# A hybrid decoder layer: the S5 setup's steps ordered behind the projection's own work on VectorE and SyncE

## The chip, the cores and the metric

The kernel runs on one core of a Trainium2 chip. The metric is the device time of one execution in microseconds (us); the number that counts is the median over runs. The core has a matrix engine (TensorE, PE in the profile, with PEld for its weight loads), three engines for elementwise work (VectorE = DVE, ScalarE = ACT, GpSimd = POOL) and SyncE (SP), which here only issues DMA transfers. Each engine runs its instructions strictly in the order of its own queue; what an instruction needs from another engine it waits for with a semaphore, and everything behind it on its queue waits too.

## The reference, cut to what matters

The layer normalises `x` (2048 tokens of 1024), projects it with one wide weight, and feeds three branches whose results are gated, projected, merged and added to `x`:

```
h = rms_norm(x, norm_w);  proj = h @ w_in
(u_a, z_a, q, k, v, z_b, xbc, dt, z_c, gate_logits) = split(proj)
y_a = s5_mixer(u_a, ...) * silu(z_a)              # diagonal complex state space model
y_b = attention_mixer(q, k, v, ...) * silu(z_b)   # 3 groups of dilated window attention
y_c = ssd_mixer(xbc, dt, z_c, ...)                # Mamba-2
merged = sum_i sigmoid(gates_i) * (y_i @ proj_i)
out = x + merged @ w_out
```

The S5 branch needs tables that depend on the parameters alone, not on `x`. The step that prepares them starts as

```
step = exp(log_step);  mag = exp(a_re * step);  ang = a_im * step
lam_re, lam_im = mag * cos(ang), mag * sin(ang)
bb = f(lam, a) * b         # (32 groups, 64 states, 16 channels), complex
```

and goes on to powers of `lam`, products with `b` and `c`, and their layout in DRAM.

## The kernel before

The projection is the first stage. `main_qkv` (L421 to L443) goes through ten weight groups of 256 columns, in the order q0, k0, v0, q1, k1, v1, q2, k2, v2, z. For each it loads 1 MB of weights (`wr`, one buffer; L370), casts it to a high part on ScalarE (`wh`, L385) and forms the low part on VectorE (`wl`, L386), in four pieces each (`wh_q_0` to `wh_q_3`). Then come four units; a unit is 48 matmuls of 128x256 (L398 to L400: high by high, low by high, high by low), three for each of 8 slices of the contraction and two token tiles, so that the pieces 0 to 3 of `wh` and `wl` are wanted one after the other. A unit's result goes from PSUM (three buffers) to SBUF by a ScalarE copy; q and k are then normalised by `head_norm` (L445 to L455: copy and square on ScalarE, sum on VectorE, two power operations on GpSimd, a multiplication on VectorE, L454), v is only copied, z gets a SiLU. A store on SyncE's queue (L442) ends the unit, and its instruction is kept in `self.anchor`. The units are numbered from 1: q0 has 1 to 4, k0 5 to 8, v0 9 to 12, q1 13 to 16, k1 17 to 20, v1 21 to 24, q2 25 to 28, k2 29 to 32, v2 33 to 36, z 37 to 40.

Beside the units other work is generated in steps. `run` takes jobs as (generator, steps, first unit, last unit) and advances each after every unit by the share that is due. In the first forty units two jobs run: `s5_setup` and `a0_early`, which normalises the second half of the tokens (`x` loads L280, `xj`, `xs`, `x`, L289 to L295, `xe`).

`s5_setup` (L1063 to L1235) loads the S5 parameters (`s5ld`, `s5prm`, `s5b`, L1075 to L1087), transposes two of them on TensorE (`s5pt`, L1079), computes exponentials, sine and cosine on 128x32 tiles, powers (`s5pw`, `s5wr`, `s5w`, L1102 to L1148), the `bb` products (`s5bb`, L1158 to L1160), loads and scales `c` (`s5c`, L1166 to L1169), transposes it on TensorE (`s5ct`, L1173) and copies it out (`s5d`, L1175), and builds two levels of phases (`s5ph`, L1182 to L1221). `put` (L1083) writes the tables to `tab_d` in DRAM: 2048 rows of 32 floats, thus 128 bytes a row and 256 KB a put, nine puts in all. The generator has fifteen points at which it yields. Its memory (a pool named `jp0`) is given back when unit 40 has been generated; attention's first loads (`qb`, `kb`, `vb`, L797) and the next step of S5, `s5_tables` (L1241 to L1306: `s5ks`, `s5x`, `s5k`, `s5o`, `s5w`, and the store `o_d<-s5o`, L1289), use the same memory, and so wait for the last put to have landed.

What is generated is not what runs. A list scheduler orders each engine's queue from a model of the time line, and may take an instruction of a step earlier than the units around it wherever its data and memory allow. `issue_after(ins)` limits that: all instructions made under it stand behind `ins` if they are on the same engine as `ins`. It orders a queue and adds no semaphore.

Of the kernel before, what the change touches and what calls it, by code (L numbers as in the profile page):

```python
# [21 lines left out]
P = 128  # L22
# [127 lines left out]
class Hybrid:  # L150
# [294 lines left out]
    def head_norm(self, nm, ps, e):  # L445
        nc = self.nc
        sq = self.ev(f"sq_{nm}")
        ss = self.gp.tile([P, 2, 8], F32, name=f"ss_{nm}", tag="hss", bufs=3)
        nc.scalar.copy(e, ps)
        e8 = e.rearrange("p a (h d) -> p (a h) d", d=64)  # L450
        nc.scalar.activation(sq.rearrange("p (h d) -> p h d", d=64), e8, AF.Square)
        nc.vector.reduce_sum(ss[:, 0, :], sq.rearrange("p (h d) -> p h d", d=64), axis=AX.X)
        self.rsqrt(ss[:, 1, :], ss[:, 0, :], 8, 1.0 / 64, EPS)
        nc.vector.tensor_mul(e8, e8,  # L454
                             ss[:, 1, :].unsqueeze(2).to_broadcast([P, 8, 64]))  # L455

    def silu2(self, nm, z, out, zin=None):

# [1083 lines left out]
    def main(self):  # L1542

        first = []
        for half, order in enumerate(((self.main_qkv, self.main_dtz, self.main_xbc, self.main_uz, self.main_gates),
                                      (self.main_uz, self.main_qkv, self.main_dtz, self.main_xbc, self.main_gates_plain))):
            for f in order:
                first.append((f, half))
        def early(gen, n):
            for _ in range(n):  # L1550
                yield next(gen)

        def chain(*gens):
            for g in gens:
                yield from g

        def steps(jobs):
            done = [0] * len(jobs)
            alive = [True] * len(jobs)

            def advance(u):
                for i, (g, n, a, b) in enumerate(jobs):
                    want = n * (u - a + 1) / (b - a) if u >= a else 0
                    while alive[i] and (done[i] < want or u >= b):
                        try:
                            next(g)
                            done[i] += 1
                        except StopIteration:
                            alive[i] = False
            return advance  # L1570

        def open_pool(name):
            st = ExitStack()
            return st, st.enter_context(self.tc.tile_pool(name=name, bufs=1, side="right"))

        def run(jobs, until):

            nonlocal u
            adv = steps(jobs)
            while u < until:  # L1580
                if next(units, 0) is None:
                    u += 1
                    adv(u)
                else:
                    break
            adv(10 ** 6)

        def all_units():
            for k, (f, half) in enumerate(first):
                if k == 0:  # L1590
                    self.a0()
                    self.consts()
                elif k == 5:
                    self.a0_late(3)
                yield from f(half)

        u, units = 0, all_units()
        st, self.jp = open_pool("jp0")
        ssd0, early0 = self.ssd(0), self.a0_early()
        run([(self.s5_setup(), 18, 2, 38), (early(early0, 6), 6, 20, 40)], 40)  # L1600
        st.close()
        tb, self.tp = open_pool("tp")
        st, self.jp = open_pool("jp1")
        tabs = self.s5_tables()
        run([(chain(self.attention(0, 0), self.attention(1, 0)), 40, 41, 79), (early(tabs, 54), 54, 41, 80),
             (self.ssd_dt(0, self.jp), 3, 73, 79), (early0, 3, 40, 52)], 80)
        st.close()
        sums = self.sums(0)
        run([(tabs, 10, 80, 86), (early(sums, 4), 4, 81, 85)], 85)
        run([(tabs, 10, 80, 86), (sums, 5, 85, 88)], 88)  # L1610
        tb.close()
        st, self.sp = open_pool("sp0")
        run([(ssd0, 65, 89, 135)], 136)
        st.close()
        st, self.jp = open_pool("jp2")
        run([(self.s5(), 42, 153, 180)], 180)
        st.close()
        st, self.jp = open_pool("jp2g")
        run([(self.s5_glu(), 25, 181, 196), (self.ssd_dt(1, self.jp), 2, 196, 198)], S5END)
        st.close()  # L1620
        self.jp = self.left_pool("jp3")
        st, self.op = open_pool("op")
        ssd, merge = self.ssd(1), self.merge()
        att = chain(self.attention(0, 1), self.attention(1, 1), self.attention(2, 1))
        run([(early(att, 46), 46, S5END + 2, 236), (self.out_weights(), 20, S5END + 3, 234)], 236)
        st.close()
        self.late = [None, None]
        self.late[0], self.sp = open_pool("sp1")
        run([(att, 26, 236, ATTEND), (early(ssd, 11), 11, 237, ATTEND)], ATTEND)
        self.close_left()  # L1630
        self.late[1], self.mp = open_pool("mp")
        run([(early(merge, 4), 4, ATTEND, 272), (early(ssd, 6), 6, ATTEND, 272)], 10 ** 6)
        self.close_left()
        self.rest = [merge, ssd]
# [51 lines left out]
```

## Time and profile before

| what | value |
|---|---|
| median of 3 runs (lowest, highest) | 2504.53 us (2504.11, 2505.44) |
| the profiled execution's own time | 2510.43 us |
| its span, first to last instruction | 2508.4 us |
| TensorE busy | 2426.4 us, 97% |
| weight loads / VectorE / ScalarE / GpSimd busy | 85% / 57% / 33% / 29% |
| mean granted TensorE clock | 0.988 |
| chain that ended last | PE 68%, DMA 12%, DVE 10%, POOL 3%, SP's queue 3%, ACT 2% |

The profiled execution took 2.0 us more than its span and 5.9 us more than the median. TensorE is busy nearly throughout, so a change in a stage can be seen in two places only: in TensorE's idle time (the view of waits, with what ended each wait) and in the granted clock (the view of windows, where 1.00 is 2.4 GHz and 0.50 is 1.2 GHz). A row of a timeline gives the start, the busy time, the engine and line, and in square brackets the idle time before it with what ended that.

### The profile page before, as it was taken

The numbers are of one execution on the slowest core, as the hardware profiler recorded it, in microseconds if no ns is written. First come the engines' busy times: TensorE is split into PE (matmuls) and PEld (weight loads), VectorE is DVE, ScalarE is ACT, GpSimd is POOL, SyncE is SP. The second block draws the span as 40 slices with busy tenths as digits, with TensorE's granted clock in tenths as the row PEclk, the third lists the DMA queues.
The fourth block names the chain that finished last, engine by engine and source line by source line (L and its number), as shares of the span: only waits on it lengthen the run. The fifth ranks groups of instructions, "written<-read, shape, count | busy, mean of one in ns | idle before, by whom it ended". The sixth has DMA issues, their size and how long they took to land.

```text
span 2508.4 us, 40680 instructions
## 1 busy us (share of the span) xinstructions
PE 2426.4 (97%) x15072; PEld 2126.8 (85%) x15072; DVE 1436.5 (57%) x3104; ACT 836.6 (33%) x1780; POOL 722.8 (29%) x785
## 2 busy tenths in 40 slices
PE   8989999999999999999999999999999799999999
PEld 8989998788788888988999978878888578898888
DVE  6953467876767672577664566632334886552321
ACT  4223334543444343222243355542332312120100
POOL 2242233543344540245331000010110465422120
PEclk9999999999999999999999999999999899999999
DMA  7764543454544456466544567783343689898886
GB/s 165 111 166 139 163 124 128 139 168 131 155 140 123 125 170 195 113 183 169 156 154 140 166 204 211 239 269 106 114 130 108 209 281 314 292 304 292 297 285 221
DMA packets 449734, 457.65 MB, mean 182 GB/s; under 512 B 115585, under 2 KB 389505, under 8 KB 442369
## 3 DMA queue, kind: packets, MB, share of 16 engines
q1 hardware_dynamic: 449536, 455.06, 59.0%
q8 instruction: 119, 1.95, 0.3%
q14 instruction: 79, 0.64, 0.1%
HBM read 306.90 MB, written 148.06 MB: 181 GB/s over the span
## 4 chain that ended last, share of the span: by engine, by line
PE 68%; DMA 12%; DVE 10%; POOL 3%; SPq 3%; ACT 2%; issue 2%; ACTq 0%; DVEq 0%; POOLq 0%
PE fp L1500 3%; PE fp L1501 3%; PE fp L1502 3%; PE ps_g L410 3%; PE ps_g L409 3%; PE ps_g L411 3%; PE ao L874 2%; PE ps_uz L409 2%; PE ps_uz L411 2%; PE ps_uz L410 2%; PE op L1531 2%; PE op L1532 2%; PE op L1533 2%; PE psx_g L722 2%; PE psx_g L720 2%
## 5 line engine op out<-in xcount | busy, mean ns | idle before, releaser
L1013 POOL TENSOR_TENSOR sr<-tle,ahl 128x384 fp32r<-128x384 f32 x128 | 126.6, 1008 | 483.9 <-PE sd L1018 400.4
L1501 PE MATMUL fp<-fy_lo,fp 128*128 128x512 f32 x384 | 154.4, 402 | 6.5 <-DVE fy_lo L1473 6.5
L1500 PE MATMUL fp<-fy_hi,fp 128*128 128x512 f32 x384 | 156.7, 409 | 0.0
L409 PE MATMUL ps_g<-hT_hi,wh_g 128*128 128x512 f32 x384 | 155.4, 405 | 0.0
L410 PE MATMUL ps_g<-hT_lo,wh_g 128*128 128x512 f32 x384 | 154.3, 402 | 0.0
L411 PE MATMUL ps_g<-hT_hi,wl_g 128*128 128x512 f32 x384 | 154.1, 401 | 0.0
L1502 PE MATMUL fp<-fy_hi,fp 128*128 128x512 f32 x384 | 153.7, 400 | 0.0
L1531 PE MATMUL op<-fo,fm_hi 128*128 128x256 f32 x512 | 146.1, 286 | 4.7 <-DMA fo<-wo_d 4.7
L1505 POOL TENSOR_TENSOR fm<-fm,fg 128x512 f32<-128x512 f32 x64 | 86.7, 1355 | 218.1 <-DVE fg L1503 153.4
L1532 PE MATMUL op<-fo,fm_hi 128*128 128x256 f32 x512 | 144.8, 283 | 0.0
L1533 PE MATMUL op<-fo,fm_lo 128*128 128x256 f32 x512 | 144.5, 283 | 0.1
L409 PE MATMUL ps_xbc<-hT_hi,wh_xbc 128*128 128x512 f32 x320 | 130.0, 406 | 0.0
L411 PE MATMUL ps_xbc<-hT_hi,wl_xbc 128*128 128x512 f32 x320 | 128.9, 403 | 0.0
L410 PE MATMUL ps_xbc<-hT_lo,wh_xbc 128*128 128x512 f32 x320 | 127.9, 400 | 0.0
L853 ACT ACTIVATE sm<-sm,ml 128x256 f32<-128x256 f32 (+1 forms) x192 | 86.3, 451 | 119.9 <-DVE ml L851 113.5
L398 PE MATMUL ps_q<-wh_q,hT_hi 128*128 128x256 f32 x384 | 112.1, 293 | 7.5 <-ACT wh_q L385 7.4
L400 PE MATMUL ps_q<-wh_q,hT_lo 128*128 128x256 f32 x384 | 109.9, 287 | 3.9 <-DVE hT_lo L331 3.9
L399 PE MATMUL ps_v<-wl_v,hT_hi 128*128 128x256 f32 x384 | 108.5, 283 | 3.2 <-DVE wl_v L386 3.2
L399 PE MATMUL ps_q<-wl_q,hT_hi 128*128 128x256 f32 x384 | 110.0, 287 | 0.9 <-DVE wl_q L386 0.9
L398 PE MATMUL ps_v<-wh_v,hT_hi 128*128 128x256 f32 x384 | 109.6, 286 | 0.0
L398 PE MATMUL ps_k<-wh_k,hT_hi 128*128 128x256 f32 x384 | 108.7, 285 | 0.0
L399 PE MATMUL ps_k<-wl_k,hT_hi 128*128 128x256 f32 x384 | 108.2, 283 | 0.2 <-DVE wl_k L386 0.2
(477 smaller groups left out, 7579.5 us busy)
## 6 DMA issues: line engine op xcount, KB each, us to landing
fp<-pw_d SPq DMA_DIRECT2D x32, 1536.0 KB, 6.7
fo<-wo_d SPq DMA_DIRECT2D x16, 2048.0 KB, 9.0
fg<-g_d SPq DMA_DIRECT2D x96, 256.0 KB, 7.0
gr<-in_w_in_dram SPq DMA_DIRECT2D x48, 256.0 KB, 3.4
wr_g<-in_w_in_dram SPq DMA_DIRECT2D x12, 1024.0 KB, 5.4
g_d<-e_g SPq DMA_DIRECT2D x48, 256.0 KB, 2.4
wr_xbc<-in_w_in_dram SPq DMA_DIRECT2D x10, 1024.0 KB, 5.7
x<-in_x_dram SPq DMA_DIRECT2D x32, 256.0 KB, 3.7
```

Of the source, the lines that this page charges most:

```text
L398: nc.tensor.matmul(ps, hi[:, t], wh, start=kt == 0, stop=False)
L399: nc.tensor.matmul(ps, hi[:, t], wl, start=False, stop=False)
L409: nc.tensor.matmul(ps, wh, hi, start=kt == 0, stop=False)
L410: nc.tensor.matmul(ps, wh, lo, start=False, stop=False)
L411: nc.tensor.matmul(ps, wl, hi, start=False, stop=kt == KT - 1)
L1013: nc.gpsimd.tensor_mul(r, self.tle.unsqueeze(1).to_broadcast([P, 3, P]), ahl[:, i, h0:h0 + 3].unsqueeze(2).to_broadcast([P, 3, P]))
L1500: nc.tensor.matmul(ps, W[k][0], yh[k], start=k == k0, stop=False)
L1501: nc.tensor.matmul(ps, W[k][0], yl[k], start=False, stop=False)
L1502: nc.tensor.matmul(ps, W[k][1], yh[k], start=False, stop=k == k1 - 1)
L1531: nc.tensor.matmul(ps, mh[k][:, t], W[k][0], start=k == 0, stop=False)
L1532: nc.tensor.matmul(ps, mh[k][:, t], W[k][1], start=False, stop=False)
L1533: nc.tensor.matmul(ps, mlo[k][:, t], W[k][0], start=False, stop=k == 7)
```

## The change

The store that ends a unit already sets `self.anchor`; now the multiplication that ends `head_norm` sets `self.anchor_v`. A wrapper, `behind`, makes each step of `s5_setup` under `issue_after` of both: the step's DMA instructions stand behind the last unit's store on SyncE's queue, and its VectorE instructions behind the last normalising multiplication on VectorE's. The v and z units have no `head_norm`, so `anchor_v` stays that of the last k unit in them. On TensorE, ScalarE and GpSimd nothing is bound. The job's numbers go from (18, 2, 38) to (18, 3, 35): the steps now follow units 3, 4, 6, 8, 10, 11, 13, 15, 17, 19, 20, 22, 24, 26 and 27, where step i followed unit 2i.

```
-        nc.vector.tensor_mul(e8, e8,
-                             ss[:, 1, :].unsqueeze(2).to_broadcast([P, 8, 64]))
+        self.anchor_v = nc.vector.tensor_mul(e8, e8,
+                                             ss[:, 1, :].unsqueeze(2).to_broadcast([P, 8, 64])).ins
...
+        def behind(gen):
+
+            while True:
+                with ExitStack() as st:
+                    st.enter_context(self.tc.issue_after(self.anchor))
+                    st.enter_context(self.tc.issue_after(self.anchor_v))
+                    try:
+                        next(gen)
+                    except StopIteration:
+                        return
+                yield
...
-        run([(self.s5_setup(), 18, 2, 38), (early(early0, 6), 6, 20, 40)], 40)
+        run([(behind(self.s5_setup()), 18, 3, 35), (early(early0, 6), 6, 20, 40)], 40)
```

On SyncE's queue the S5 transfers move. Around the turn from v0 to q1 (`wr_k_0_1781` is the weight load of k1; `v_d` and `q_d` are unit stores, `tab_d` the puts, `s5c` the loads of `c`) the queue of before has:

```order
L442 DMA v_d_69<-e_v_0_1_1251 128x2x256
L1083 DMA tab_d<-s5bb_1402 2048x1x32
L1083 DMA tab_d<-s5bb_1408 2048x1x32
L442 DMA v_d_69<-e_v_1_0_1347 128x2x256
L442 DMA v_d_69<-e_v_1_1_1399 128x2x256
L370 DMA wr_k_0_1781<-in_w_in_dram 128x8x256
L442 DMA q_d_64<-e_q_0_0_1481 128x2x256
```

and the queue of after, in the same place:

```order
L442 DMA v_d_69<-e_v_0_1_1251 128x2x256
L1140 DMA rho_d<-s5sv 128x32
L1083 DMA tab_d<-s5wr 2048x1x32
L1083 DMA tab_d<-s5w 2048x1x36
L442 DMA v_d_69<-e_v_1_0_1347 128x2x256
L1083 DMA tab_d<-s5bb_1350 2048x1x32
L1083 DMA tab_d<-s5bb_1356 2048x1x32
L370 DMA wr_k_0_1781<-in_w_in_dram 128x8x256
L442 DMA v_d_69<-e_v_1_1_1411 128x2x256
L442 DMA q_d_64<-e_q_0_0_1481 128x2x256
L1166 DMA s5c_1491<-in_s_c_re_dram 128x4x64
L1167 DMA s5c_1492<-in_s_c_re_dram 128x4x64
```

Two puts (`s5wr`, `s5w`) that stood ahead of v0's first store stand behind its second, close to the `s5bb` puts, and the four loads of `c`, which stood in the queue ahead of the first store of all, stand behind the store of q1's first unit.

On TensorE the eight transposes of `c` (`s5ct`) stood in the last unit of q0, at the turn to the first units of k0:

```order
L399 MATMUL ps_q_1_1_636<-wl_q_0_3_234,hT_1_hi 128x256
L400 MATMUL ps_q_1_1_636<-wh_q_0_3_233,hT_1_lo 128x256
L1173 MATMUL s5ct_1558<-ident,s5c_1550 128x128 x3
L1173 MATMUL s5ct_1566<-ident,s5c_1551 128x128 x4
L398 MATMUL ps_k_0_0_788<-wh_k_0_2_780,hT_1_hi 128x256
```

and stand now inside the last unit of q1, behind 11 and 15 of its 48 matmuls:

```order
L398 MATMUL ps_q_1_1_1722<-wh_q_0_1_1420,hT_0_hi 128x256
L399 MATMUL ps_q_1_1_1722<-wl_q_0_1_1421,hT_0_hi 128x256
L1173 MATMUL s5ct_1499<-ident,s5c_1491 128x128 x4
L400 MATMUL ps_q_1_1_1722<-wh_q_0_1_1420,hT_0_lo 128x256
L398 MATMUL ps_q_1_1_1722<-wh_q_0_2_1424,hT_1_hi 128x256
L399 MATMUL ps_q_1_1_1722<-wl_q_0_2_1425,hT_1_hi 128x256
L400 MATMUL ps_q_1_1_1722<-wh_q_0_2_1424,hT_1_lo 128x256
L1173 MATMUL s5ct_1507<-ident,s5c_1492 128x128 x4
L398 MATMUL ps_q_1_1_1722<-wh_q_0_2_1424,hT_1_hi 128x256
```

They moved by about a whole round of q, k and v.

On VectorE the operations of `s5_tables` that wait for the memory of `s5_setup` (`s5x`, `s5k`, `s5w`) stood ahead of the last two low weight pieces of q2:

```order
L1263 TENSOR_TENSOR s5x_3695<-s5x_3695,s5xt_3696 128x256
L1263 TENSOR_TENSOR s5k_3706<-s5k_3706,s5kt_3707 128x256
L1305 TENSOR_TENSOR s5w_3909<-s5w_3909,s5wt_3910 128x2x256
L1263 TENSOR_TENSOR s5o_3825<-s5o_3825,s5ot_3826 128x256
L1305 TENSOR_TENSOR s5w_3909<-s5w_3909,s5wt_3910 128x2x256
L1263 TENSOR_TENSOR s5x_3920<-s5x_3920,s5xt_3921 128x256
L290 TENSOR_TENSOR xs_2619<-xs_2619 128x1
L295 TENSOR_SCALAR x_0_2270<-x_0_2270,xs_2619 128x512
L295 TENSOR_SCALAR x_1_2271<-x_1_2271,xs_2619 128x512
L386 TENSOR_TENSOR wl_q_0_2_2466<-wr_q_0_2455,wh_q_0_2_2465 128x2x256
L386 TENSOR_TENSOR wl_q_0_3_2470<-wr_q_0_2455,wh_q_0_3_2469 128x2x256
```

and stand now ahead of those of v2 (`wr_v_0_3080` is v2's weight):

```order
L454 TENSOR_TENSOR e_k_0_1_2922<-e_k_0_1_2922,ss_k_0_1_2924 128x512
L1263 TENSOR_TENSOR s5x_3695<-s5x_3695,s5xt_3696 128x256
L1263 TENSOR_TENSOR s5k_3706<-s5k_3706,s5kt_3707 128x256
L452 TENSOR_REDUCE ss_k_1_0_3013<-sq_k_1_0_3012 128x8
L1305 TENSOR_TENSOR s5w_3909<-s5w_3909,s5wt_3910 128x2x256
L386 TENSOR_TENSOR wl_v_0_2_3091<-wr_v_0_3080,wh_v_0_2_3090 128x2x256
L386 TENSOR_TENSOR wl_v_0_3_3095<-wr_v_0_3080,wh_v_0_3_3094 128x2x256
```

The last two puts of `s5ph` moved with them: on SyncE's queue they stood between k1's second and third store and stand now between q2's third and fourth. From about unit 41 on the queues are the same until the last stage, in which the instructions of the second half's SSD, the merge and the output projection interleave in another order on every engine.

## Rows read from the trace of the kernel before

**Rows 1.** The page, part 1: busy us (share of the span) and instructions

```profile
PE 2426.4 (97%) x15072; PEld 2126.8 (85%) x15072; DVE 1436.5 (57%) x3104; ACT 836.6 (33%) x1780; POOL 722.8 (29%) x785
```

**Rows 2.** TensorE's waits, 0 to 320 us: total us, times, longest

```profile
PE ps_q L398 <- ACT wh_q L385: 7.4, 2, 6.8
PE ps_q L400 <- DVE hT_lo L331: 3.9, 1, 3.9
...
PE ps_v L399 <- DVE wl_v L386: 3.2, 3, 1.7
...
PE ps_q L399 <- DVE wl_q L386: 0.9, 2, 0.5
```

**Rows 3.** Windows: us, PE, PEld, DVE, ACT, POOL busy (count), clock, DMA, GB/s

```profile
174.00:177.00 3.00, 0.00 (x0) 0.00 (x0) 1.26 (x1) 0.80 (x3) 2.10 (x3) 0.55 0.94 304
177.00:180.00 3.00, 1.65 (x6) 1.35 (x6) 1.40 (x4) 2.12 (x5) 0.75 (x2) 0.50 0.79 286
180.00:183.00 3.00, 2.70 (x12) 2.70 (x13) 2.05 (x3) 0.00 (x0) 2.47 (x2) 0.50 0.29 55
183.00:186.00 3.00, 3.00 (x22) 3.00 (x21) 1.02 (x2) 0.00 (x0) 1.06 (x1) 0.74 1.06 341
186.00:189.00 3.00, 3.00 (x28) 3.00 (x27) 1.72 (x3) 2.26 (x4) 0.00 (x0) 1.00 0.55 215
```

**Rows 4.** The chain that ended last, 140 to 186 us: start, us, what

```profile
146.44 10.61 DMA tab_d<-s5ph
...
171.97 0.32 SPq L1289
172.34 3.78 DMA x<-in_x_dram
...
179.65 0.61 DVE wl_q L386
```

**Rows 5.** VectorE's timeline, two rows of 155 to 182 us

```profile
157.24 0.24 DVE L1281 MEMSET s5ks<- 16x224 f32 x1 [7.41 <-DMA k_d<-e_k]
...
169.07 1.53 DVE L1305 TENSOR_TENSOR s5w<-s5w,s5wt 128x512 f32<-128x512 f32 x1 [1.97 <-POOL s5wt L1304]
```

**Rows 6.** Windows, the start of the projection

```profile
27.00:30.00 3.00, 2.36 (x11) 2.36 (x12) 2.65 (x6) 0.48 (x1) 0.74 (x2) 0.59 0.86 267
```

**Rows 7.** SyncE's queue, 80 to 120 us

```profile
84.80 0.51 SPq L1083 DMA_DIRECT2D tab_d<-s5w  x1
...
90.13 3.81 SPq L1083 DMA_DIRECT2D tab_d<-s5bb  x2
...
98.87 0.42 SPq L370 DMA_DIRECT2D wr_k<-in_w_in_dram  x1
115.12 0.36 SPq L442 DMA_DIRECT2D q_d<-e_q  x1
```

**Rows 8.** ScalarE's timeline: the high weight pieces of k1

```profile
107.32 1.15 ACT L385 CAST wh_k<-wr_k 128x512 fp32r<-128x512 f32 x2 [8.93 <-DMA wr_k<-in_w_in_dram]
```

**Rows 9.** Windows, longer ones: v0 to q1, and v1 to q2

```profile
84.00:105.00 21.00, 21.00 (x180) 21.00 (x180) 19.99 (x119) 4.41 (x8) 0.00 (x0) 1.00 1.17 145
140.00:160.00 20.00, 17.62 (x148) 17.21 (x147) 9.89 (x32) 4.27 (x9) 7.09 (x6) 1.00 0.81 131
```

**Rows 10.** DMA issues of 0 to 180 us: count, KB each, median us to landing

```profile
tab_d<-s5ph SPq DMA_DIRECT2D x4, 256.0 KB, 8.5
...
s5c<-in_s_c_im_dram SPq DMA_DIRECT2D x2, 128.0 KB, 6.8
```

**Rows 11.** TensorE's timeline: a wait in v0, the start of k1, a wait in v1

```profile
76.85 0.39 PE L399 MATMUL ps_v<-wl_v,hT_hi 128*128 128x256 f32 x1 [0.78 <-DVE wl_v L386]
...
120.27 0.28 PE L398 MATMUL ps_k<-wh_k,hT_hi 128*128 128x256 f32 x1
...
147.06 0.38 PE L399 MATMUL ps_v<-wl_v,hT_hi 128*128 128x256 f32 x1 [1.73 <-DVE wl_v L386]
```

**Rows 12.** TensorE's waits from 1960 us to the end

```profile
PE fp L1501 <- DVE fy_lo L1473: 6.5, 3, 4.7
```

## The prediction

> **What bounds the kernel now.** I first read the shares: TensorE is busy for 97% of the span [rows 1], so the reader should ask where it idles and where its clock falls. The list of TensorE's waits in the first 320 us, where the S5 setup runs, answers the first: 7.4 us for the high weight pieces of q (one wait of 6.8), 3.9 at the start for `hT_lo`, 3.2 in three waits for low pieces of v, 0.9 for low pieces of q [rows 2]. The windows answer the second: around the 6.8 us wait the granted clock falls to 0.55 and then 0.50 (1.2 GHz); a window at 0.50 holds 12 matmuls, the next one 22 and a full one 28 [rows 3]. Together with a 0.48 us wait right behind, that stall is 7.2 us of idleness and some (28−12)/28 × 3 us of the one slow full window, plus (28−22)/28 × 3 in the next, 1.7 + 0.6, and nearly 1 us in the window before, where PE was busy 1.65 us with 6 matmuls for what takes 0.7: about 3.2 us in all. The stall costs **10.4 us**.
>
> The chain shows its cause. The last put of `s5ph` left at 146.44 and took 10.61 us; behind it VectorE's L1281 started at 157.24, after 7.41 us of idleness [rows 4, 5]. The tables' operations follow one another up to the store L1289 (171.97), behind which the `x` loads stood (172.34, 3.78 us), and behind these the norm of `x`, and the low pieces of q2 (179.65) [rows 4]. The high pieces wait in the same convoy. So it is not that work is lacking: S5's tables and the weights share in-order queues at the turn from one user of a memory to the next.
>
> **The change part by part.** No arithmetic is added or removed; all terms are waits. Times are those of before, shifted by what comes earlier.
>
> *The stall at q2 goes.* The last puts stand behind q2's third store, so `qb` and L1281 can't hold up q2: −10.4. Of the 3.2 us in v, 0.78 stands in v0; the other 2.4, 1.73 of them in one wait, stand in v1 [rows 2, 11] and came from low pieces of v1 behind the last phase operations, which have moved on: −2.4; the clock there was 1.00 throughout [rows 9], so nothing more comes back. Removed: **−12.8**.
>
> *The same transition now stands at v2.* The last phase operation is behind q2's third normalisation; replaying VectorE's queue from the start of q2 (call it U), I put it at U+28. The put lands 8.5 to 10.6 us later [rows 4, 10], L1281 starts at about U+38, and from L1281 to the end of `s5w`, behind which the low pieces 2 and 3 of v2 now stand, it took 157.24 to 170.6, 13.4 us [rows 5]; the piece itself adds 0.7. That is U+51 to U+54. TensorE wants it at U+49 (eight units of 5.7 us, and 12 matmuls of the ninth, with some 2 us lost before). A new wait of 1.5 to 6, taken as 4.5, and 0 to 3.2 for the clock, taken as 2.5 (an idleness of 3.9 at the start was followed by a window at 0.59, one of 1.73 by none) [rows 2, 6, 9]: **+7.0**, between +1.5 and +9.5.
>
> *The transposes of `c` become a wait.* This is the largest term. Before, one put and the next left up to 84.8, two more from 90.1, and the weights of k1 at 98.87; ScalarE had them at 107.32 after 8.93 us of waiting [rows 7, 8]. Now all four puts stand closely ahead of that load, and their sources on VectorE come later, because VectorE was already full there (19.99 of 21 us, with the DMA engines above 1.0 of their share) [rows 9]. I put the load at 100 to 107 and its landing at 108 to 116. ScalarE's copy of q1's first unit stands behind the cast of these weights; 7.8 us after the cast began (107.32 to 115.12) came that unit's store [rows 7, 8], and behind this store stand now the four loads of `c`. They are issued over 2 to 4 us and land in 3.8 (what an `x` load took) to 6.8 us (what they took) [rows 4, 10], then VectorE scales them: the transposes are ready at 115 + 3 + 3.8 + 0.4 = 122 at the earliest, and at 133 if the weights come late and the landing is slow. TensorE's queue reaches them 11 matmuls into q1's last unit, which starts 5.7 us before k1 at 120.27 [rows 11]: at 116.0, or 118.5 with what is lost before. In the order of before they stood in q0 and had their data at once. The wait is 3.5 to 14, taken as 9, and the clock costs 0 to 3.2, taken as 2.5, because nothing else feeds TensorE meanwhile: **+11.5**.
>
> Here a page of the Trainium skill would price it otherwise. "DMA: Bandwidth & Descriptors", section "Anatomy of one DMA — SWDGE (gpsimd) path", gives a fit of 2.0 us plus bytes over 436 GB/s per transfer, measured on another issue path; by it a put of 256 KB is 2.6 us. By this rule the four puts don't delay the weights, the wait is at its low end of 3.5, and v2 has none: 0.7 + 1.8 + 0.5 + 3.5 + 1.7 − 12.8 = −4.6. Its section "Specifications" says that below 512 bytes a piece the engines read, modify and write, and lose line rate; a put here is 2048 pieces of 128 bytes and took 10.61 us [rows 4], so the trace bears out the second section and not the first.
>
> *VectorE early.* The weights of k0 now leave ahead of `x` loads at the start; setup operations that were taken early now come when the units need VectorE for low pieces. At the start (+0.7), in v0 (+1.8 beyond the 0.8 that it waits now) and in q1 (+0.5); the nearest row is the wait of 3.9 at the start, where TensorE stood behind such a VectorE queue [rows 2]. **+3.0**, between 0 and +8.
>
> *q2's own start.* Its low pieces stand behind `x` loads that stand behind two puts: **+1.7**, between 0 and +5 (a put of 8.5 and a load of 3.8, less what v1 covers) [rows 4, 10].
>
> *The last stage.* The queues interleave otherwise on all engines, with the same work. I see no reason for a sign; single waits there are up to 4.7 [rows 12]. 0, with ±5.
>
> Sum: −12.8 + 7.0 + 11.5 + 3.0 + 1.7 = **+10.4**. The profiled execution took 2510.4 us, so I expect about 2520.8 for one under the profiler, and against the median of 2504.5, **2514.9**. All low ends give −12.8 + 1.5 + 3.5 = −8, all high ends −12.8 + 9.5 + 17.2 + 8 + 5 = +27, the last stage aside.
>
> **The rivals.** A difference of 0.2% (5.0 us) is about what a measurement of this kernel can tell from none: faster means below 2499.5, slower above 2509.5.
>
> *Faster.* The removed stall is not replaced: the puts land before k1's weights, the transposes wait 3 us without loss of clock, and v2 waits 1.5 or not at all. −12.8 + 3 + 1.5 + 1.5 = −7, 2497.7. For it: before, weights behind two puts landed in 8.5 us [rows 7, 8]. Against it: now there are four puts, and the store that frees the loads of `c` was at 115.1 even then. It holds if the transposes' data is there by 119. 17%. Of these 17, 4 are for the Trainium skill's fit above, as the 10.61 us speak against it.
>
> *No change.* The stall is spread over shorter waits that leave the clock at 1.00: v0 2, `c` 4.5, q2 1.7, v2 3.5: 11.7 − 12.8 = −1, 2503. The row for it is that 1.73 us cost no clock [rows 9, 11]. 24%.
>
> *Much slower.* The four puts hold k1's weights to 116 or later; q1's last unit then waits for a free PSUM buffer and for the transposes, 14, and k1's own start is late; the full clock loss twice and v2 at 6: −12.8 + 14 + 3.2 + 9.2 + 3 + 1.7 = +18, 2522.8. It decides itself at the issue of k1's weights: beyond 106 us. 17%.
>
> *The change doesn't do what it says.* TensorE isn't bound, so the scheduler could have kept the transposes early; the order shows it did not. What remains is that the setup is moved without any effect at the units, and the last stage's order alone decides: ±5 around −1 to +3. 6%, half of it slower.
>
> **How the numbers follow.** My forecast, 2510 to 2520 around 2514.9, has 36%; much slower 17%, faster 17%, no change 24%, no effect 6%. Slower: 36 + 17 + 3 and 1 of the no-change case that ends over the bound, 57%; same: 25%; faster: 18%. The range leaves out the fastest tenth (below 2498.5) and the slowest tenth (above 2526).
>
> **What would show it.** In the profile of after: no wait of `ps_q` for `wh_q` at 170 us; a wait of TensorE at L1173 or just behind it, at 116 to 133 us, ended by the scaling L1168 or the loads of `c`, with a granted clock of about 0.5 behind it; k1's weight load at SyncE after 100 us; a wait of `ps_v` for `wl_v` at about 230 to 240 us ended by VectorE. If the first is gone and the second is under 4 us, my largest term is wrong and the result is near the second rival; if the high pieces at q2 still wait, the convoy was not the cause; if all early waits come out as written and the time differs by more than 5 us, the last stage decided.

## The result and the profile after

The change made the kernel slower, and by more than I had said. In the first comparison the median went from 2504.99 to 2529.71 us, a ratio of 1.0097 (95% interval 1.0079 to 1.0115): 24.7 us, where I had forecast +10.4 with a range up to 2526. The changed kernel run again in a later comparison took 2529.52 beside 2511.73 for the kernel before, 1.0069 (1.0053 to 1.0085): 17.8 us. The two profiled executions differ by 17.0 us of span (2508.4 and 2525.4). So the direction held, the size did not.

The page of after, part 1, answers to [rows 1]: 9.2 us more of TensorE being busy with the same 15072 matmuls, some of which ran at the lower clock, and 7.8 us more idleness.

```profile
PE 2435.6 (96%) x15072; PEld 2135.8 (85%) x15072; DVE 1446.3 (57%) x3104; ACT 835.3 (33%) x1780; POOL 722.2 (29%) x785
```

TensorE's waits of after, 0 to 340 us, in the columns of [rows 2]. The long wait for the high pieces at q2 has halved (6.8 to 3.4), the waits of v1 are gone, and two new ones head the list: the transposes of `c` and the low pieces of v, which are v2's now.

```profile
PE s5ct L1173 <- DVE s5c L1168: 7.6, 1, 7.6
PE ps_v L399 <- DVE wl_v L386: 5.7, 1, 5.7
PE ps_q L398 <- ACT wh_q L385: 3.8, 2, 3.4
...
PE ps_q L400 <- DVE hT_lo L331: 2.7, 1, 2.7
...
PE ps_q L398 <- ACT e_q L449: 1.8, 1, 1.8
```

The windows of after show what [rows 3] showed at q2: around the 7.65 us wait the clock is at 0.50 (1.2 GHz), and it is back at 1.00 in the window from 126 us; behind v2's wait it is at 0.50 too.

```profile
114.00:117.00 3.00, 1.10 (x10) 0.89 (x8) 0.79 (x2) 2.35 (x5) 1.83 (x2) 0.71 0.00 0
117.00:120.00 3.00, 0.00 (x0) 0.00 (x0) 1.19 (x2) 0.00 (x0) 1.64 (x2) 0.50 0.41 124
120.00:123.00 3.00, 0.26 (x1) 0.26 (x2) 0.60 (x2) 0.00 (x0) 0.19 (x1) 0.50 0.61 138
123.00:126.00 3.00, 3.00 (x17) 3.00 (x17) 2.21 (x5) 0.00 (x0) 1.61 (x2) 0.59 0.28 93
126.00:129.00 3.00, 3.00 (x28) 3.00 (x27) 2.35 (x12) 1.24 (x2) 0.22 (x1) 1.00 0.97 128
...
237.00:240.00 3.00, 2.94 (x13) 2.94 (x14) 1.80 (x3) 0.00 (x0) 2.83 (x5) 0.50 0.25 43
```

The chain to the transposes, first in SyncE's timeline (answers to [rows 7]), then in ScalarE's (answers to [rows 8]), last in TensorE's. The weight load of k1 leaves at the same time as before, but its issue is drawn out to 3.87 us and ScalarE gets the weights at 111.86 instead of 107.32; q1's first store follows at 117.66, the loads of `c` behind it, and TensorE's transposes at 122.74.

```profile
93.99 4.82 SPq L1083 DMA_DIRECT2D tab_d<-s5bb  x2
98.90 3.87 SPq L370 DMA_DIRECT2D wr_k<-in_w_in_dram  x1
...
117.66 0.36 SPq L442 DMA_DIRECT2D q_d<-e_q  x1
118.07 0.46 SPq L1166 DMA_DIRECT2D s5c<-in_s_c_re_dram  x1
```

```profile
111.86 1.14 ACT L385 CAST wh_k<-wr_k 128x512 fp32r<-128x512 f32 x2 [16.46 <-DMA wr_k<-in_w_in_dram]
```

```profile
113.53 0.38 PE L398 MATMUL ps_q<-wh_q,hT_hi 128*128 128x256 f32 x1 [1.75 <-ACT e_q L449]
122.74 1.12 PE L1173 MATMUL s5ct<-ident,s5c 128*128 128x128 f32 x4 [7.65 <-DVE s5c L1168]
```

The load that left on time landed late. These are the DMA issues of after from 85 to 110 us, in the columns of [rows 10]; the put of `s5w` has 36 floats a row and 288 KB, unlike the others, and `s5_setup` has ten puts, not nine.

```profile
wr_k<-in_w_in_dram SPq DMA_DIRECT2D x1, 1024.0 KB, 12.9
...
tab_d<-s5bb SPq DMA_DIRECT2D x2, 256.0 KB, 13.2
tab_d<-s5w SPq DMA_DIRECT2D x1, 288.0 KB, 9.8
tab_d<-s5wr SPq DMA_DIRECT2D x1, 256.0 KB, 6.5
```

To see where all 17.0 us lie I read from TensorE's timelines when each group of units starts (its first matmul), here with the experiments of below. "last" is the first matmul of the last stage (`fp`), "length" the span from there to the end.

```
kernel            v0     q1     k1     v1     q2     k2     v2     z      last    length  span
before            73.9   97.6  120.3  143.4  169.8  203.8  227.3  251.6  1978.4  530.0   2508.4
changed           71.6   94.6  129.3  152.0  175.7  205.8  229.3  261.7  1988.9  536.5   2525.4
e1                74.3   97.0  120.0  151.8  180.6  215.3  238.8  263.6  1987.3  538.7   2526.0
e2                72.9   95.6  129.1  151.8  175.3  206.1  229.6  262.2  1988.7  527.7   2516.4
e3                73.0   95.7  119.3  143.6  173.0  206.7  230.2  254.6  1981.1  529.4   2510.5
e4                72.6   96.8  130.9  153.5  177.1  207.0  230.4  266.5  1993.3  535.3   2528.6
e5 changed again  71.7   95.3  131.5  154.3  177.8  208.5  232.0  265.1  1993.2  537.0   2530.2
e6                72.7   96.2  123.2  147.3  170.8  197.2  220.7  256.4  1988.1  537.7   2525.8
e7                74.2   96.9  119.6  142.9  170.5  194.1  217.6  242.0  1979.2  532.5   2511.7
e8                74.2   96.9  119.5  142.6  168.7  198.7  222.2  246.5  1970.7  530.6   2501.3
e9                73.0   96.4  123.2  146.0  175.7  205.5  229.0  261.9  1990.2  536.1   2526.3
e10               72.9   95.6  128.1  150.8  174.3  200.7  224.2  260.6  1993.0  531.6   2524.6
e11               72.2   95.8  128.9  151.8  179.1  202.6  226.1  258.9  1989.9  535.4   2525.3
e12               74.6   97.7  120.4  143.8  169.5  195.5  219.0  243.4  1967.3  529.3   2496.6
```

At z the changed kernel is 10.1 us late, at the last stage 10.5, and the last stage itself takes 6.5 us more. In the windows of the last stage, before and after, in the columns of [rows 3], TensorE is busy for 510.4 and 511.6 of 530.0 and 536.5 us, so 5.3 of the 6.5 us are idleness:

```profile
1978.40:2508.40 530.00, 510.41 (x2999) 445.21 (x2998) 257.69 (x442) 78.70 (x148) 180.03 (x157) 0.98 0.82 283
1988.90:2525.40 536.50, 511.62 (x2999) 445.36 (x2998) 260.89 (x442) 78.50 (x148) 178.75 (x157) 0.98 0.81 279
```

A single execution is one draw. The changed kernel's second profile, e5, reaches z 13.5 us later than before and the last stage 14.8 later, but takes 537.0 us for the last stage, nearly what the first took.

TensorE's list of waits there has two of over 2 us that before had not: 5.4 us for `fm_lo` (L1533), with matmuls of 0.41 instead of 0.28 us behind it, and 2.3 for `fg` (L1500). In exchange the wait for `wo_d` is shorter. First two rows of before from 1960 us ([rows 12] stands between them), then those of after from 1980 us; the waits for `sx`, all but 1.8 and 0.5 us of them, stand ahead of the stage's first matmul:

```profile
PE spt L1059 <- DVE sx L1053: 8.1, 2, 6.3
...
PE op L1531 <- DMA fo<-wo_d: 4.7, 3, 2.8
```

```profile
PE spt L1059 <- DVE sx L1053: 6.7, 2, 6.2
PE fp L1501 <- DVE fy_lo L1473: 6.2, 2, 5.7
PE op L1533 <- DVE fm_lo L1513: 5.4, 1, 5.4
...
PE op L1531 <- DMA fo<-wo_d: 2.5, 1, 2.5
...
PE fp L1500 <- DVE fg L1503: 2.3, 2, 2.0
```

### The profile page after: what moved, and what is told of

It is laid out like the page before. It is cut to its first block, busy times and chain, and to the rows that moved or that the text cites. A ratio compares the mean times of both kernels' runs of the same rounds, so it can differ in the third digit from the quotient of the medians.

```text
span 2525.4 us, 40681 instructions
## 1 busy us (share of the span) xinstructions
PE 2435.6 (96%) x15072; PEld 2135.8 (85%) x15072; DVE 1446.3 (57%) x3104; ACT 835.3 (33%) x1780; POOL 722.2 (29%) x785
## 4 chain that ended last, share of the span: by engine, by line
PE 73%; DMA 10%; DVE 8%; SPq 3%; POOL 2%; ACT 2%; issue 2%; DVEq 0%; ACTq 0%; POOLq 0%
PE ps_g L409 3%; PE ps_g L410 3%; PE ps_g L411 3%; PE fp L1500 3%; PE fp L1502 3%; PE fp L1501 3%; PE ao L874 3%; PE ps_xbc L409 3%; PE ps_xbc L411 2%; PE ps_xbc L410 2%; PE op L1533 2%; PE op L1531 2%; PE op L1532 2%; PE ps_uz L409 2%; PE ps_uz L411 2%; PE ps_uz L410 2%
## 5 line engine op out<-in xcount | busy, mean ns | idle before, releaser
L1500 PE MATMUL fp<-fy_hi,fp 128*128 128x512 f32 x384 | 157.3, 410 | 2.7 <-DVE fg L1503 2.3
L1533 PE MATMUL op<-fo,fm_lo 128*128 128x256 f32 x512 | 145.2, 285 | 5.5 <-DVE fm_lo L1513 5.4
L400 PE MATMUL ps_v<-wh_v,hT_lo 128*128 128x256 f32 x384 | 110.4, 288 | 0.0
```

Of the source, the lines that this page charges most:

```text
L400: nc.tensor.matmul(ps, lo[:, t], wh, start=False, stop=kt == KT - 1)
L1500: nc.tensor.matmul(ps, W[k][0], yh[k], start=k == k0, stop=False)
L1533: nc.tensor.matmul(ps, mlo[k][:, t], W[k][0], start=False, stop=k == 7)
```

## The experiments

Four questions: is the loss of the last stage its own or only the early one seen again; what makes the wait for the transposes; which half of the binding does it; and is the convoy that I read at q2 really what stalls q2. The expectations were written against 2505 and 2529.7; each time is to be compared with that of before in its own comparison, which stands beside it.

**The last stage: a cross of two by two.** Its queues come in two versions, that of before and that of after, and which one the scheduler makes turned out to hang on one binding: that of the first step's loads on SyncE's queue. e1 has only this binding, e2 has all others. Both in `behind`:

```
e1:  +                    if j in [1]:
                              st.enter_context(self.tc.issue_after(self.anchor))
     -                    st.enter_context(self.tc.issue_after(self.anchor_v))
e2:  +                    if j in [2, 3, ..., 16]:
                              st.enter_context(self.tc.issue_after(self.anchor))
                          st.enter_context(self.tc.issue_after(self.anchor_v))
```

> The kernel with the new ramp, but only the first step of the S5 setup (the loads of s5ld, s5prm, s5b) is bound, and only on SyncE's queue. The early queues stay near those of the kernel before (transposes of c in q0, the stall at q2 kept), while the last stage gets exactly the order of the changed kernel. Theory A (the last stage's order costs what the early waits don't explain): 2505 + 7 to 14, thus 2512 to 2519, with TensorE reaching z within 3 us of before and the last stage longer by 7 to 14. Rival B (the order of the last stage is worth nothing; all 24.7 us come from the first 260 us): 2502 to 2508.

> The changed kernel with one binding taken away: the first step's loads are free on SyncE's queue. The early part keeps the late transposes of c and the transition at v2, the last stage gets the order of the kernel before. Theory A: the early part costs 10 and the last stage nothing, 2505 + 10 = 2515, range 2512 to 2519. Rival B: 2527 to 2532, as the changed kernel.

e1 took 2529.00 us beside 2510.54 of before (ratio 1.0067, 1.0043 to 1.0092), e2 2521.78 (1.0040, 1.0026 to 1.0053). As to the last stage theory A holds on both: e1 needs 538.7 us for it, e2 527.7. As to the early part e1 was a miss: I had expected it near the kernel before, and it reaches z at 263.6, 12 us late, with no wait at the transposes but one of 7.17 at k1, one of 3.71 at v1 and one of 8.37 at q2. One moved group of loads costs as much there as the whole change. In e1 too the four puts stand closely ahead of k1's weight load (its issue takes 3.37 us, ScalarE has the weights at 112.54), and TensorE meets the delay although the transposes ran early.

All other kernels but one fall into the same two classes. With the order of before (before, e2, e3, e8, e10, e12) the last stage takes 527.7 to 531.6 us, mean 529.8; with the order of after (changed twice, e1, e4, e6, e9, e11) 535.3 to 538.7, mean 536.7. The ranges do not meet, whatever the early part did. e7 has a third order, with 532.5 us. The wait that goes with the order of after, 5.3 to 5.6 us at the same matmul (`op` on `fm_lo`), is in all seven profiles of that class and in none of the six of the other; this is e1's:

```profile
2108.19 0.80 PE L1533 MATMUL op<-fo,fm_lo 128*128 128x256 f32 x2 [5.64 <-DVE fm_lo L1513]
```

In VectorE's timeline of the changed kernel one sees what `fm_lo` stands behind: the merge's `my` products, low parts `fy_lo` of the next tokens, and a step of the SSD state. So far the cause is shown as the order of the stage as a whole; that this one wait makes most of the 6.9 us between the means is a reading of these rows, which no run tested by itself.

```profile
2100.28 2.43 DVE L910 TENSOR_TENSOR my<-moa,msc 128x256 f32<-128x256 f32 x2
2102.75 1.12 DVE L912 TENSOR_TENSOR my<-my 128x256 f32<-128x256 f32 x1
2103.80 2.23 DVE L1473 TENSOR_TENSOR fy_lo<-fy,fy_hi 128x512 fp32r<-128x512 f32 x1
2105.95 0.54 DVE L1044 TENSOR_TENSOR ssd_state<-ssd_state,ssp 128x384 f32<-128x384 f32 x1
2106.41 1.18 DVE L910 TENSOR_TENSOR my<-mob,msc 128x256 f32<-128x256 f32 x1
2107.52 1.02 DVE L1473 TENSOR_TENSOR fy_lo<-fy,fy_hi 128x512 fp32r<-128x512 f32 x1
2108.46 0.41 DVE L912 TENSOR_TENSOR my<-my 128x256 f32<-128x256 f32 x1
2108.79 0.68 DVE L1513 TENSOR_TENSOR fm_lo<-fm,fm_hi 128x512 fp32r<-128x512 f32 x1
```

**What makes the wait for the transposes.** e3 binds only the step of `c`, and only on SyncE's queue (`if j in [7]`). e4 is the changed kernel with the four loads of `c` moved from that step to the first:

```
         nc.vector.tensor_scalar(bb[1][0:64], bb[1][0:64], -1.0, None, op0=ALU.mult)
+        c = [self.ct(f"s5c{i}", [P, 4, 2, 64]) for i in range(2)]
+        for i, w in enumerate(("s5_c_re", "s5_c_im")):
+            ...  # the four loads, as they stood
         yield
```

> The kernel before with only the step of c bound on SyncE's queue: its loads stand behind the store of q1's first unit, the transposes in q1's last unit; the stall at q2 stays possible and the last stage keeps the order of before. Theory A (the wait for the transposes stands by itself): 8 us of idleness and 3 of clock, 2516, range 2512 to 2519. Rival C (what TensorE loses there it gets back, because the convoy of puts and tables that stalls q2 by 10.4 us runs on meanwhile): the stall at q2 shrinks by as much and the time is 2504 to 2508.

> The changed kernel with the four loads of c put into the first step, beside those of b: the transposes then have their data, and everything else is as in the changed kernel, its order of the last stage too. Theory A (the wait for the transposes stands by itself): the wait of 7.6 us at L1173 and its clock go, 2529.7 - 11 = 2519, range 2515 to 2522. Rival C (what is gained is lost again at q2 and v2, whose transition does not depend on TensorE): these waits grow by 8 to 11 and the time is 2526 to 2531.

Both were misses. e3 took 2511.19 (0.9998, 0.9985 to 1.0010), but not as rival C has it: the wait did not come at all. The loads of `c` did stand behind q1's first store, yet the weights of k1 were there at 102.50, the store left at 109.72, and the transposes ran without waiting:

```profile
116.10 0.60 PE L1173 MATMUL s5ct<-ident,s5c 128*128 128x128 f32 x4
117.62 0.60 PE L1173 MATMUL s5ct<-ident,s5c 128*128 128x128 f32 x4
```

e4 took 2530.55 (1.0068, 1.0042 to 1.0094), and its wait stayed, 8.81 us, though its loads had landed long before. VectorE's scaling L1168 now stood behind q1's first normalisation, and that behind k1's weights, cast at 113.47:

```profile
119.46 1.97 PE L1173 MATMUL s5ct<-ident,s5c 128*128 128x128 f32 x8 [8.81 <-DVE s5c L1168]
```

So the place of the loads alone neither makes the wait nor is needed for it. What the two have apart is when k1's weights land, because ScalarE's copy of q1's first unit stands behind their cast. e9 tests that alone: in the changed kernel the two puts of `s5bb` go behind the loads of `c`; no other row of any engine's queue moves.

```
-            put(64 + 16 * i, 16, o.rearrange("p (b g) k -> p b (g k)", b=16))
+            bo.append(o)
         yield
...
             put(96 + 16 * i, 16, d.rearrange("p a (h c) -> p (a h) c", h=4))
+        for i, o in enumerate(bo):
+            put(64 + 16 * i, 16, o.rearrange("p (b g) k -> p b (g k)", b=16))
         yield
```

> The changed kernel with one thing moved: the two puts of s5bb stand behind the loads of c instead of ahead of k1's weight load. The orders of TensorE, VectorE, ScalarE and GpSimd stay as they are. Theory D (k1's weights land late because the puts are ahead of them in the DMA rings, and everything behind the first q1 normalisation comes late with them): the cast of k1's high pieces starts near 105 to 107 instead of 112, the wait at L1173 falls from 7.6 to 1 to 4, and TensorE starts z 5 to 9 us sooner. Rival (the weights wait for something else, the buffer or the store before): the cast stays at 110 or later and the wait at 6 or more; z starts within 2 us of the changed kernel. In the median the gain is 0 to 7 by D, since part of a gain there was given back in the freed-step run.

Theory D holds at its place. The weights leave at 97.84 with an issue of 0.38 us instead of 3.87, ScalarE has them at 107.03 instead of 111.86, their landing takes 9.1 us instead of 12.9, and the wait falls from 7.65 to 3.09:

```profile
107.03 1.15 ACT L385 CAST wh_k<-wr_k 128x512 fp32r<-128x512 f32 x2 [9.88 <-DMA wr_k<-in_w_in_dram]
```

```profile
117.91 0.65 PE L1174 MATMUL s5ct<-ident,s5c 128*128 128x128 f32 x4 [3.09 <-DVE s5c L1169]
```

k1 starts at 123.2 instead of 129.3. But the weights of v1 come hardly earlier (ScalarE casts them at 138.05, in the changed kernel at 139.22), so TensorE meets a new wait of 3.10 for v1's low pieces, and at z nothing is left (261.9 and 261.7; 265.1 in e5). That part of theory D, 5 to 9 us at z, was a miss; the time is 2529.06 (1.0078, 1.0061 to 1.0096). e6 is the changed kernel with the step of `c`, number 7, bound on neither queue:

> The changed kernel with the whole step of c unbound, on SyncE's and on VectorE's queue: its loads, transposes and puts go back to q0's end as before, the rest stays, the last stage's order too. Theory A (the wait for the transposes stands by itself): 11 us less than the changed kernel. Theory D (what delays q1 is k1's weight load landing late behind the puts of s5wr, s5w and s5bb; the transposes only pass it on to TensorE): TensorE meets a wait for a free PSUM buffer or for k1's weights of 2 to 5 us instead, and the gain is 5 to 9. Rival C (given back at q2 and v2): 0 to 3 less.

The transposes go back to q0 and their wait is gone; in its place TensorE waits 2.61 us for a PSUM buffer and 1.21 for k1's low pieces, as D has it:

```profile
116.03 0.58 PE L398 MATMUL ps_q<-wh_q,hT_hi 128*128 128x256 f32 x1 [2.61 <-ACT e_q L449]
128.22 0.39 PE L399 MATMUL ps_k<-wl_k,hT_hi 128*128 128x256 f32 x1 [1.21 <-DVE wl_k L386]
```

z comes at 256.4, 8.7 us before that of the changed kernel of the same comparison (265.1), but the first matmul of the last stage only 5.1 before, and the median is 2527.01 (1.0055, 1.0041 to 1.0070) against the 2529.52 of e5. So the waits are those of theory D, but the gain of 2.5 us is what rival C had. Where the other 3.6 us went between z and the last stage I did not settle. e5 is the changed kernel, unedited, in that comparison:

> The changed kernel as it is, beside the kernel before on the same chip, to have both on one chip and a second profile. If the difference of 24.7 us is the change's own, it is 20 to 28 again; if part of it lay in that chip's runs, it is what the two profiled executions differ by, 15 to 19.

17.8 us in the medians, as the two profiled executions said; so some 7 of the first comparison's 24.7 us belong to its runs of before, whose median of 2504.99 no later comparison repeated (2510.54, 2511.73 and 2509.93).

**Which half.** e10 binds the steps on VectorE's queue alone (the line with `self.anchor` taken out), e11 on SyncE's alone (the line with `self.anchor_v` taken out).

> One half of the change: the steps are bound on VectorE's queue alone; SyncE's queue is free. The last stage has the order of the kernel before, the transposes of c stand in the third unit of q1, the transition to s5_tables at v2. If the wait for the transposes comes with VectorE's binding (the scaling of c stands behind q1's first normalisation): a wait at L1173 of 5 to 9, z at +8 to +12, and 8 to 12 us over before. If it comes with SyncE's: no such wait, only the transition at v2 (5 to 9 us) in place of the one at q2 (10), and the time within 4 us of before.

> The other half: the steps are bound on SyncE's queue alone. The last stage has the changed order. If VectorE's binding makes the wait for the transposes: no wait over 2 us at L1173, z at 0 to +5, and the last stage's 7 to 8 on top, 7 to 13 over before. If SyncE's binding makes it: z at +8 to +12 and 15 to 20 over before.

I had written these as if one of the two were the cause. Either half suffices: the wait at the transposes is 6.51 us in e10 and 7.18 in e11, ended by VectorE's scaling each time. In both the four puts stand closely ahead of k1's load and ScalarE has the weights late (109.96 and 110.91).

```profile
115.95 1.97 PE L1173 MATMUL s5ct<-ident,s5c 128*128 128x128 f32 x8 [6.51 <-DVE s5c L1168]
```

e10, with the last stage's order of before, took 2521.41 (1.0047, 1.0031 to 1.0063), e11, with that of after, 2528.37 (1.0063, 1.0038 to 1.0088), beside 2509.93: 11.5 and 18.4 us over before.

**The convoy at q2.** e7 leaves `s5_setup` as before and holds the steps that follow unit 40, `s5_tables` and attention, behind z's last unit, on SyncE's and VectorE's queues; e8 does so on VectorE's alone; e12 on VectorE's, and on GpSimd's behind the last normalisation of k2 (`self.anchor_k`, the second power operation there; the lines that set it are left out).

```
+        self.anchor_z = nc.vector.scalar_tensor_tensor(out, t, 1.0, ...).ins      # silu2
...
+        at_z = (self.anchor, self.anchor_z)         # e8: (self.anchor_z,)
+        tabs = held(self.s5_tables(), at_z)         # e12: (self.anchor_z, self.anchor_k)
-        run([(chain(self.attention(0, 0), self.attention(1, 0)), 40, 41, 79)
+        run([(held(chain(self.attention(0, 0), self.attention(1, 0)), at_z), 40, 41, 79)
```

> The kernel before with another cure for the stall at q2: the steps of s5_tables and of attention that follow unit 40 are bound behind z's last unit on SyncE's and VectorE's queues, so that no operation that waits for the S5 setup's memory stands ahead of q2's, k2's and v2's work. If the convoy is the cause: TensorE starts z 10 us sooner than in the kernel before (near 241), with no wait over 2 us at q2; the time is 5 to 12 us below before if the late tables cost nothing, unless the last stage, whose order is a third one here, costs up to 8. If the transition costs the same wherever it stands, z starts early and the wait shows up at the first units after z.

> As the run before, but only on VectorE's queue; the last stage has the order of the kernel before. If VectorE's table operations ahead of q2's low weight pieces are what makes the stall: the wait at q2 falls from 6.8 to under 3 us and the time is 4 to 10 us below before. If GpSimd's and SyncE's part of the convoy (the qb loads, s5x) makes it: the stall stays above 5 and the time within 3 us of before.

> The kernel before with the steps of s5_tables and attention behind unit 40 bound on VectorE's queue (behind z's last unit) and on GpSimd's (behind the last normalisation of k2), SyncE's free; the last stage has the order of before. Against the run that held VectorE alone, the s5x products leave GpSimd's queue between the normalisations of k1 and q2: if they made the 2.7 us that were left at q2, that wait is under 1.5 and the time another 2 to 4 us lower, 6 to 10 below before; if not, the same within 2 us.

In e7 there is no wait at q2, and z starts at 242.0, 9.6 us before that of the kernel before, nearly the 10.4 that I had read from [rows 2, 3]. All of it is given back at once: the tables, now late on SyncE's queue, hold up the norm of `x` behind GpSimd's products, and TensorE waits 6.63 us at 287; the time is 2513.72 (1.0002, 0.9991 to 1.0014), where I had expected a gain if the late tables cost nothing.

```profile
287.27 1.97 PE L301 MATMUL xT<-ident,x 128*128 128x128 f32 x8 [6.63 <-DVE x L295]
```

e8, which lets the loads go early, keeps 2.69 us of the wait at q2 and takes 2507.92 (0.9977, 0.9966 to 0.9988), 3.8 below before and just short of the 4 that I had expected at least. e12 also takes the products out of GpSimd's way: 0.75 and 1.15 are left at q2, and no new wait over 0.7 us comes later (to 340 us). It takes 2504.70 beside 2509.93 (0.9974, 0.9962 to 0.9987): the best of all, 5.2 us better than the kernel before, where I had expected 6 to 10. Between e8 and e12, which ran in two comparisons, the ratios can't tell, and the profiled spans, 2501.3 and 2496.6, differ by less than the runs of either do among themselves.

```profile
171.85 0.51 PE L398 MATMUL ps_q<-wh_q,hT_hi 128*128 128x256 f32 x2 [0.75 <-ACT wh_q L385]
173.98 0.39 PE L399 MATMUL ps_q<-wl_q,hT_hi 128*128 128x256 f32 x1 [1.15 <-DVE wl_q L386]
```

## Why the prediction was wrong, point by point

**The last stage, the term that failed.** I had seen that its queues come out in another order and wrote 0 with ±5, "no reason for a sign". It measured +6.5 in the two profiled executions, +6.9 between the means of the two classes. My bound came from a single wait in the stage of before, 4.7 us [rows 12] (the same list has a longer one, 6.3, just ahead of the stage); but another order makes its own wait (5.3 to 5.6 at L1533), and slower matmuls behind it. The forecast for a profiled execution was 2520.8 and it took 2527.1: the 6.3 that were missing are the size of this term.

**From the profiled execution to the median.** I carried over the 5.9 us by which the profiled execution of before lay above the median of three runs. In the three later comparisons, on three chips, the median of before was within 1.3 us of that profiled execution (2510.43); the three runs had been low. So 2514.9 was some 6 us too low for all but the first comparison, and there the changed kernel did not share the low level: its median, 2529.7, lay 2.6 above its profiled execution. Of the 14.8 us between 2514.9 and 2529.7 this step thus has 8.5 and the last stage 6.3. Why the first comparison's runs of before were low is open. Against 2511.73, beside the changed kernel run again, 7.4 us are missing (17.8 instead of 10.4), and there the last stage is nearly all.

**The sum of the early part was right, by luck: two of its terms were not.** +10.4 was forecast, +10.1 measured at z (13.5 in e5). e2, which has the early part without the new order of the last stage, is 11.2 over before in the median. But the first and the third term below are off by −6.0 and +4.5 us, and these errors nearly cancel.
- *VectorE early*: +3.0 forecast, −3.0 measured at the start of q1 (94.6 and 97.6). The wait for `hT_lo` was 2.68 instead of 3.89, and v0's wait was gone. I counted only work that comes later, not what it may free at the start. How much of it the change makes is not shown, as the start varies by itself: that wait was 2.4 to 4.4 in all kernels that I ran, and q1 starts at 95.7 to 97.7 in e3, e7, e8 and e12, in which the setup's first six steps are not bound.
- *Transposes of `c`*: +11.5 forecast, 12.0 measured (q1 to k1 took 34.7 instead of 22.7 us), with 7.65 of idleness, 1.75 for the PSUM buffer and half the clock. The size was right, and the route in part: I had put the lateness on the puts ahead of k1's weights, which e9 confirmed, and on the loads of `c` behind the store, which e3 and e4 showed to be neither enough nor needed. The load of the weights left at 98.9, before the 100 to 107 that I had given; it was its landing that was late.
- *q2*: −12.8 + 1.7 = −11.1 forecast, −6.6 measured (v1's start to k2's: 53.7 instead of 60.4 us). The transition left, but its place was taken by a wait of 3.42 for the norm of `x`, whose load took 8.9 us on the chain, right behind SyncE's two puts of the first level; I had given that 1.7 and no clock. By my own sign, high pieces still waiting at q2 meant that the convoy was not the cause; the sign was too blunt, since a different wait came to the same place, and e7, e8 and e12 show the convoy to be the cause of the stall of before.
- *v2*: +7.0 forecast, +8.1 measured. The wait is where and what I had said: L1281 starts at 220.09 by the landing of `tab_d`, `s5w` at 234.88, the low piece behind it, 5.67 us.

**The rivals.** *Much slower* (2522.8) was nearest in time and wrong in part of its mechanism: TensorE did wait for a PSUM buffer and for the transposes, but 9.4 us and not 14, and k1's weights did not leave after 106 but at 98.9, and arrived late because of the puts ahead of them. *Faster* is out: the transposes' data was there at 122.7 and not by 119. With it goes the price that my prediction took from the Trainium skill, "DMA: Bandwidth & Descriptors" ("Anatomy of one DMA — SWDGE (gpsimd) path"), whose fit makes a put an estimated 2.6 us. The four puts took 6.5 to 14.2 us each from issue to landing, and the 1 MB load behind them 12.9; with two of them moved away (e9) it took 9.1. *Doesn't do what it says* was out by the order, and right in one point, that the last stage's order decides.

**The range.** The sum of all high ends, +27, reached 2531.5 even without the last stage, and so beyond 2529.7; but I cut the range at 2526, the slowest tenth. The last stage's ±5 went into no sum and the step from the profiled execution to the median had no range at all, so that tenth was drawn too low.

## What to carry to other kernels

When a scheduler makes the queues, a binding at the start can reorder a stage two milliseconds later: compare the whole order, and price each reordered stage by itself, best by finding a variant that has the one and not the other. A wait that is taken from one place in a chain of in-order queues is often not gained but met again further down (e7, e9); what helped (e8, e12) was to take the waiting operations out of the queue of the engine that feeds TensorE, and to leave the loads early. And a forecast against a median of three runs needs the spread between comparisons in its range.

## What the runs showed of the hardware

- A put of 2048 pieces of 128 bytes, 256 KB, delays a transfer behind it: with four of them closely ahead (one of 288 KB), the issue of a 1 MB weight load took 3.87 us and its landing 12.9, and ScalarE stood idle for 16.46 us until it had the weights; with two of the puts moved away the issue took 0.38 us, the landing 9.1, and the weights were there 4.8 us sooner (e9).
- The kernel before, unchanged, had medians of 2504.99, 2510.54, 2511.73 and 2509.93 us in four comparisons, and single runs from 2503.78 to 2520.8. Differences of under 5 us need both kernels side by side on one chip, and several runs of each.
